# Layer 1's projections of the normalised input: fp16 pairs scaled on the chip in place of fp32r pairs

## The chip, the cores and the metric

The kernel runs on one core of one Trainium2 chip. The metric is the device time of one execution in microseconds (us); lower is better. TensorE is called PE in the profile (its weight loads PEld), VectorE DVE, ScalarE ACT, GpSimd POOL, and SyncE, which here only issues DMAs, SP.

## The reference, cut to what matters

Two layers of a diffusion trunk on 512 latent and 256 context tokens, 1024 channels. Each layer normalises its input, modulates it, multiplies it by one wide matrix `w_in` (1024 x 5376), runs two attentions (a neighbourhood attention A and a grouped-query attention B, 8 heads of 64 each), gates both, and projects twice.

```python
for l in range(2):
    mod_x = silu(c) @ w_ada + b_ada                       # likewise mod_c for the context
    hx = rmsnorm(x, norm_g) * (1 + scale_x) + shift_x      # hc for the context
    a_k, a_v, b_k, b_v, a_q, b_q, a_z, b_z, g_a, g_b = split(hx @ w_in)
    ca_k, ca_v, cb_k, cb_v = split(hc @ w_in)              # layer 1 needs no more of the context
    qa, ka, qb, kb = rmsnorm of each head of a_q, a_k, b_q, b_k (rotary on b)
    a_att, b_att = attention A, attention B
    o_a, o_b = (a_att * silu(a_z)) @ w_o_a, (b_att * silu(b_z)) @ w_o_b
    x = x + gate_x * ((sigmoid(g_a) * o_a + sigmoid(g_b) * o_b) @ w_out)
```

Everything is float32; the output is the latent stream after layer 1.

## The kernel before

To keep the accuracy of float32, each product of two matrices is three matmuls: each operand is split into a rounded part `hi` and a remainder `lo = value - hi`, and `mm3` adds hi*hi, hi*lo and lo*hi in one PSUM bank (L435, L436, L437). For all projections both parts are fp32r; for the attention values they are fp16 already.

Weights come in tiles of 128 x 512 float32. `load_w` (512 columns at once, one tile for each 128 rows) and `load_w2` (256 columns, two row blocks in one tile) issue the DMA from SP into one of three `raw` buffers (L403, L417), cast `whi` on ACT (L405, L420) and subtract `wlo` on DVE or POOL (L408, L422). `mix_lo` gives every second tile to POOL; `bq_lo` every fourth. There are eight `whi` and eight `wlo` buffers.

The input of a layer's projections, `hx`, is made by `make_hx` and `turn_hx`: one token tile at a time is normalised, transposed on PE, modulated on ACT (`modc` holds shift and scale by channel) and split by DVE (L350, L351). It takes four of the nine `big` buffers, two for `hi` and two for `lo`.

Two helpers run the projections. `tok_proj` has 128 tokens stationary and 512 or 256 weight columns moving, 24 matmuls a tile (8 row blocks, 3 each). `chan_proj` has 128 weight columns stationary and the tokens moving. In layer 1 these are: `a_k`, `a_v` (6 token tiles each, 512 wide), `b_k` with `b_v` (6 tiles, 256 wide), `a_q`, `b_q` (4 tiles each, 512 wide), and 24 pieces of `chan_proj`, 512 wide, for `a_z`, `b_z`, `g_a`, `g_b`.

A layer goes through these stages: A's projections; attention A, with gate pieces as filler on PE (`fill`, run by `pipeline`); the projections of B (`w = load_w2(W, C_BKV...)`, then `b_q`); attention B with more filler; and the merge, in which `o_chunks("b")` is projected by pieces, `evac_b` gates and adds on DVE, casts `mh` on ACT (L1223) and subtracts `ml` on DVE (L1224), and `w_out` is applied to the result (`tok_proj(w, 512, a_m, ...)`), in two halves of 512 columns. During layer 0's merge the modulation of layer 1 is computed on DVE from weights in `rawb` (`ada_steps`, L297; DMAs from POOL's queue, L290), ending in `ada_mod(1)`; while the second half of `w_out` runs, `make_hx(1, ...)` makes layer 1's input.

The program is recorded in this order, and a scheduler then sets the order of each engine's instructions from its own estimate of their times, bound by data, buffers and the few orders that `behind` fixes. An engine executes its own list in order.

`shrink`, `size` and `halves` exist before: for the attention values they find the largest magnitude over all partitions (a transpose and a one-column matmul on PE, five small DVE steps) and scale a tile so that it fits fp16.

Of the kernel before, what the change touches and what calls it, by code (L numbers as in the profile page):

```python
# [72 lines left out]
def hybrid_kernel(es: ExitStack, tc, x, ctx, cvec, w_ada, w_ada0, small, gvec, w_in, w_o_a, w_o_b, w_out,  # L73
# [112 lines left out]
    ehalf = cp.tile([128, 32], F32, name="ehalf")  # L186
    G.memset(ehalf, -0.5)

# [39 lines left out]

    modc = cp.tile([128, 2, 2, 16], F32, name="modc")

    def mod_finish(l, sums, k0, k1):
# [46 lines left out]
    def ada_steps(l, tiles, halves, nv, pool, queue=None):  # L278
# [58 lines left out]
    def turn_hx(l, t, y, h, hx, pool):  # L337

        v = 0 if t < 4 else 1
        full = pool.tile([128, 4, 128], F32, tag="half", name=nm("half"), bufs=2)  # L340
        pt = psw(512, "t")
        for k in range(4):
            T.transpose(pt[:, 128 * k:128 * k + 128], y[:, 512 * h + 128 * k:512 * h + 128 * k + 128], ident)
        for k in range(4):
            kk = 4 * h + k
            S.activation(full[:, k, :], pt[:, 128 * k:128 * k + 128], AF.Identity,
                         bias=modc[:, l, v, kk:kk + 1], scale=modc[:, l, v, 8 + kk:9 + kk])
        hi = hx[0][h].rearrange("p (k n) -> p k n", k=4)[:, :, 128 * t:128 * t + 128]
        lo = hx[1][h].rearrange("p (k n) -> p k n", k=4)[:, :, 128 * t:128 * t + 128]
        V.tensor_copy(R(hi), full)  # L350
        V.tensor_tensor(R(lo), full, hi, ALU.subtract)  # L351

# [43 lines left out]

    def load_w(src, col0, n, nk, lo_eng, k0=0, own=None, bufs=8):

        pool, x = (wp, "") if own is None else (own, "x")
        res = []  # L400
        for k in range(k0, k0 + nk):
            raw = raw_tile()
            nc.sync.dma_start(raw[:, :n], src[128 * k:128 * k + 128, col0:col0 + n])  # L403
            hi = pool.tile([128, 512], F32R, tag="whi" + x, name=nm("whi"), bufs=bufs)
# [7 lines left out]
    def load_w2(src, col0, nk, lo_eng):  # L412

        res = []
        for i in range(nk // 2):
            raw = raw_tile()
            nc.sync.dma_start(raw.rearrange("p (k n) -> p k n", k=2),  # L417
                              src[256 * i:256 * i + 256, col0:col0 + 256].rearrange("(k p) n -> p k n", k=2))
            hi = wp.tile([128, 512], F32R, tag="whi", name=nm("whi"), bufs=8)
            S.copy(hi, raw)  # L420
# [18 lines left out]
    def tok_mm(ps, w, n, a, t, k0, k1):  # L439
        for k in range(k0, k1):  # L440
            hi, lo = a(0, k), a(1, k)
            mm3(ps, (R(hi[:, 128 * t:128 * t + 128]), R(lo[:, 128 * t:128 * t + 128])),
                (w[k][0][:, :n], w[k][1][:, :n]), k == 0, k == KT - 1)
# [8 lines left out]
    def chan_proj(w, f, a, n0, n1, evac, late=0):  # L452
# [4 lines left out]
        wh = lambda k, i: w[k][i][:, 128 * f:128 * f + 128]  # L457
        act = lambda k, i: R(a(i, k)[:, n0:n1])
        for k in range(late):
# [34 lines left out]
    def open_heads(stack, name, bufs):  # L494
# [3 lines left out]
        for sq in hp["sq"]:  # L498
            V.memset(sq[:, :, HD:HD + 1], HD * EPS)

    def head_ss(ps, nh, ss):
# [93 lines left out]
    def layer(l, hx, nxt, start):  # L595
        first = l == 0
        ntok = NTOK if first else NLAT
        qt = 6 if first else 4
        a_hx = lambda part, k: hx_k(hx, part, k)
        spans = [(0, 512), (512, 768)] if first else [(0, 512)]  # L600
# [17 lines left out]
        def fill_chunks(col0, dst, spill, silu, eng):  # L618

            def evac(f, n0, n1, ps):  # L620
                if spill is None:
                    d = dst().rearrange("p (f n) -> p f n", f=4)[:, f, n0:n1]
                else:
                    d = ztp.tile([128, 512], F32, tag="zt", name=nm("zt"))[:, :n1 - n0]
                S.activation(d, ps, AF.Tanh, scale=0.5)  # L625
                if silu:
# [4 lines left out]
            for i in range(2):  # L631
                st = {}

                def ld(i=i, st=st):
                    st["w"] = load_w2(W, col0 + 256 * i, KT, eng)
                res.append((ld, [lambda f=f, n0=n0, n1=n1, i=i, st=st:
# [40 lines left out]
        def o_chunks(br, prepare, evac):  # L677

            src = (w_o_a if br == "a" else w_o_b)[l]
            act = lambda part, k: gated[br][part][:, k, :]  # L680
            res = []
# [53 lines left out]
        else:  # L735
            open_heads(bgp_es, f"cp{l}", 1)
            w = load_w(W, C_AK, 512, KT, mix_lo)
            hp["lag"] = 2
# [15 lines left out]
        def split_va():  # L754
            V.tensor_reduce(vmx[:, 6:7], vmx[:, 0:6], AX, ALU.max)
            shrink(vmx[:, 6:7], vsa, vsa[0:1, 2:3], 0.5 / P_UP)
            for t in range(0, 6, 2):
                halves(vf[:, t:t + 2, :].rearrange("p t (h d) -> p (t h) d", d=64),
                       va[:, t:t + 2].rearrange("p t h q d -> p (t h) q d"), vsa[:, 0:1])
        w = load_w(W, C_AV, 512, KT, mix_lo)  # L760
        for t in range(6):
# [8 lines left out]
        qav = big("qa").rearrange("p (j n) -> p j n", j=4)  # L770
        w = load_w(W, C_AQ, 512, KT, mix_lo, own=hp["p"])
        za = big("za")
# [18 lines left out]
        if True:  # L791
# [305 lines left out]
            def split_vb():  # L1097
                size(vf.rearrange("p t n -> p (t n)"), vbig[:, 1152:1920], vbig[:, 2946:2947])
                shrink(vbig[:, 2946:2947], vs, vbig[0:1, 2948:2949], 0.5)
                halves(vf.rearrange("p t (h d) -> p (t h) d", h=2), vb.rearrange("p t h q d -> p (t h) q d"),  # L1100
                       vs[:, 0:1])

            bg = gate_steps((0,), hp["p"]) if first else []
            w = load_w2(W, C_BKV, KT, mix_lo)
            w_q = []

            def load_q():
                w_q.extend(load_w(W, C_BQ, 512, 4, bq_lo) + load_w(W, C_BQ, 512, 4, bq_lo, 4, hp["p"], 4))
            if first:
# [98 lines left out]
        with tc.tile_pool(name=f"mrg{l}", bufs=1, reuse_waits="tile") as mp:  # L1208
# [33 lines left out]
            a_m = lambda part, k: mg[k // 4][part][:, k % 4, :]  # L1242
            bg = ada_steps(1, range(16), (1,), 2, mp, G) + [lambda: ada_mod(1)] if first else []
            run(bg, 1)
# [285 lines left out]
```

## Time and profile before

| | |
|---|---|
| three runs | 1105.44, 1108.48, 1111.61 us (median 1108.48) |
| the profiled execution | 1111.07 us, of which the span is 1109.3 us |
| granted TensorE clock, mean | 0.991 |
| PE, PEld busy | 1075.5 us (97%), 879.1 us (79%) |
| DVE, ACT, POOL busy | 767.4, 617.1, 473.1 us |
| DMA | 171.79 MB, mean 155 GB/s |

A row of a group names the line, the engine, the operation, the tiles (out<-in, buffer numbers left out) and the form, then the count, the busy time, the mean of one, and the idle time ahead of it with what ended it. In a timeline, a row has the start, the time that it took, and the same names; neighbours of one kind are merged with their count. The end of a matmul is modelled, so matmuls overlap in it: the distance between two starts is the cost of one, not its duration. In a table of windows, each row has a stretch, the busy time of each engine with its instructions, the granted clock, the mean busy share of the 16 DMA engines and what they moved.

### The profile page before, as it was taken

How to read it: one execution, taken by the hardware profiler on the slowest of the kernel's cores; microseconds unless marked ns; L12 is line 12 of the kernel's file. 1: busy time of each engine (PE TensorE's matmuls, PEld its weight loads, DVE VectorE, ACT ScalarE, POOL GpSimd, SP SyncE). 2: the span in 40 equal slices, each digit the busy share in tenths (PEclk: the TensorE clock that was granted, in tenths of full speed). 3: DMA queues.
4: the chain of work that ended last, by engine and by line, in shares of the span. 5: the costliest groups of instructions: out<-in, count | busy, mean ns of one | idle time of the engine just before them, and what ended most of it. 6: DMA issues, size and time to landing. Idle time of an engine off the chain costs nothing. (4 is left out here: it accounts for less than half of the span.)

```text
span 1109.3 us, 16937 instructions
## 1 busy us (share of the span) xinstructions
PE 1075.5 (97%) x5672; PEld 879.1 (79%) x5672; DVE 767.4 (69%) x1600; ACT 617.1 (56%) x1236; POOL 473.1 (43%) x397
## 2 busy tenths in 40 slices
PE   8999999999999989989999999999999999999998
PEld 5688888788888868767788878888877888777677
DVE  4667889975377487766777785366997665677473
ACT  6454279776433566765330275444899446786430
POOL 1054235555257154463621354232355472564531
PEclk9999999999999999998999999999999999999999
DMA  9455324554543379789633542453565536879642
GB/s 370 146 171 153 90 68 111 128 138 120 169 131 127 100 184 215 166 228 228 213 101 124 157 147 78 140 163 101 134 149 130 156 107 171 199 229 239 188 152 77
DMA packets 236000, 171.79 MB, mean 155 GB/s; under 512 B 160140, under 2 KB 201864, under 8 KB 234248
## 3 DMA queue, kind: packets, MB, share of 16 engines
q1 hardware_dynamic: 228576, 156.31, 51.6%
q0 software_dynamic: 2368, 7.87, 2.1%
q10 hardware_dynamic: 4968, 6.53, 1.8%
q8 instruction: 45, 0.74, 0.3%
q14 instruction: 43, 0.35, 0.1%
HBM read 115.58 MB, written 17.32 MB: 120 GB/s over the span
## 5 line engine op out<-in xcount | busy, mean ns | idle before, releaser
L842 POOL TENSOR_TENSOR h<-p,h 128x256 f16<-128x256 f32 (+2 forms) x104 | 113.6, 1101 | 160.0 <-ACT h L841 117.7
L422 POOL TENSOR_TENSOR wlo<-raw,whi 128x512 fp32r<-128x512 f32 x70 | 98.0, 1406 | 131.6 <-ACT whi L420 98.7
L435 PE MATMUL psf<-hx,whi 128*128 128x512 f32 (+1 forms) x360 | 138.2, 384 | 2.2 <-DVE zt L627 1.2
L436 PE MATMUL psf<-hx,whi 128*128 128x512 f32 (+1 forms) x360 | 136.1, 378 | 0.0
L437 PE MATMUL psf<-hx,wlo 128*128 128x512 f32 (+1 forms) x360 | 136.1, 378 | 0.0
L435 PE MATMUL psx<-whi,hx 128*128 128x512 f32 (+1 forms) x328 | 121.0, 372 | 0.0
L437 PE MATMUL psx<-whi,hx 128*128 128x512 f32 (+1 forms) x328 | 120.0, 367 | 0.0
L420 ACT CAST whi<-raw 128x512 fp32r<-128x512 f32 x136 | 83.2, 620 | 65.5 <-DMA raw<-in_w_in_dram 46.9
L436 PE MATMUL psx<-wlo,hx 128*128 128x512 f32 (+1 forms) x328 | 119.6, 366 | 0.0
L408 POOL TENSOR_TENSOR wlo<-raw,whi 128x512 fp32r<-128x512 f32 x40 | 59.8, 1499 | 117.7 <-ACT whi L405 74.6
L405 ACT CAST whi<-raw 128x512 fp32r<-128x512 f32 x88 | 54.3, 623 | 96.7 <-PE psx L437 34.2
L508 POOL TENSOR_TENSOR ss<-ss,ehalf 128x8 f32<-128x8 f32 (+2 forms) x40 | 63.6, 1593 | 77.2 <-DVE ss L505 72.2
L841 ACT CAST h<-p 128x256 f16<-128x256 f32 (+2 forms) x136 | 81.7, 616 | 5.3 <-DMA ht<-h 1.3
L422 DVE TENSOR_TENSOR wlo<-raw,whi 128x512 fp32r<-128x512 f32 x66 | 65.3, 992 | 25.9 <-ACT whi L420 24.3
L1161 DVE CUSTOM_DVE_ANT_0 p<-pss,vb 128x768 f32<-128x768 f32 x64 | 60.2, 953 | 31.0 <-PE pss L891 28.9
L1162 ACT ACTIVATE p<-pss,mx 128x768 f32<-128x768 f32 x64 | 57.6, 901 | 41.1 <-DVE mx L1161 40.4
L435 PEld LDWEIGHTS psf<-hx,whi 128*128 128x128 f32 x360 | 68.3, 190 | 14.9 <-ACT zt L625 1.9
L437 PEld LDWEIGHTS psf<-hx,wlo 128*128 128x128 f32 x360 | 68.2, 190 | 12.0
L436 PEld LDWEIGHTS psf<-hx,whi 128*128 128x128 f32 x360 | 68.3, 190 | 10.9
L437 PEld LDWEIGHTS psx<-whi,hx 128*128 128x128 f32 x328 | 61.9, 189 | 10.2
L436 PEld LDWEIGHTS psx<-wlo,hx 128*128 128x128 f32 x328 | 62.0, 189 | 9.5
L435 PEld LDWEIGHTS psx<-whi,hx 128*128 128x128 f32 x328 | 61.8, 189 | 9.1 <-issue 0.2
(338 smaller groups left out, 2984.7 us busy)
## 6 DMA issues: line engine op xcount, KB each, us to landing
raw<-in_w_in_dram SPq DMA_DIRECT2D x168, 256.0 KB, 3.0
rawb<-in_w_ada_dram SPq DMA_DIRECT2D x48, 256.0 KB, 2.8
raw<-in_w_out_dram SPq DMA_DIRECT2D x32, 256.0 KB, 2.9
tg<-gs SPq DMA_DIRECT2D x4, 1536.0 KB, 9.9
rawx<-in_w_ada_dram SPq DMA_DIRECT2D x4, 1024.0 KB, 10.3
rawy<-in_w_ada_dram SPq DMA_DIRECT2D x4, 1024.0 KB, 10.3
gs<-zt ACTq DMA_DIRECT2D x16, 256.0 KB, 2.6
raw<-in_w_o_a_dram SPq DMA_DIRECT2D x16, 256.0 KB, 3.1
```

Source lines behind the costliest of these rows:

```text
L405: S.copy(hi[:, :n], raw[:, :n])
L408: e.tensor_tensor(lo[:, :n], raw[:, :n], F(hi[:, :n]), ALU.subtract)
L420: S.copy(hi, raw)
L422: lo_eng(i).tensor_tensor(lo, raw, F(hi), ALU.subtract)
L435: T.matmul(ps, lhs[0], rhs[0], start=first, stop=False)
L436: T.matmul(ps, lhs[0], rhs[1], start=False, stop=False)
L437: T.matmul(ps, lhs[1], rhs[0], start=False, stop=last)
L508: G.tensor_tensor(ss, ss, ehalf[:, :n], ALU.pow)
L841: S.copy(h[:, 0], p[:, :n])
L842: eng.tensor_tensor(h[:, 1], p[:, :n], h[:, 0], ALU.subtract)
L1161: V.tensor_tensor_reduce(p, pss, lift, -1.0, 3e38, ALU.add, ALU.min, mx[:, 0:1])
L1162: S.activation(p, pss, AF.Exp, bias=mx[:, 0:1], accum_out=r[:, i:i + 1])
```

## The change

In layer 1 alone, `hx` and the weights of all its projections become pairs of fp16 tiles. Since fp16 has a narrow range, both are multiplied by a scale ahead of the split. The scale of the weights comes from a bound on them: ACT reads all of `w_in[1]` during layer 0, 64 blocks of 128 x 672, and adds up their magnitudes along each row (`bound_steps`); 36 blocks are read during layer 0's projections of B and 28 during its merge, and the largest row sum gives `s_w`. The scale of `hx` comes from the sum of the magnitudes of layer 1's modulation (`scale_mod`), and is multiplied into `modc`. Their product is divided out where it matters: in the scale of `Tanh`, in the scales of the values, and in the `eps` of the head norms (`set_eps`).

A weight tile is cast and scaled by one ACT instruction; the remainder is one `scalar_tensor_tensor` on DVE, or on POOL a `tensor_scalar` in place and then the subtraction. `hx` takes two `big` buffers in place of four. The blocks of the bound are read into a `big` buffer during B's projections and into an `extra` tile of the merge, four slots of each, by DMAs that ACT issues. The `rawb` tiles of the merge get four buffers in place of two.

```diff
+    s_w, dq = ehalf[:, 24:28], ehalf[:, 28:31]
+    def bound_steps(a, b, pool, space):
+        n = b - a
+        sums = pool.tile([128, n + 1], F32, tag="wsum", name=nm("wsum"), bufs=1)
+        def step(i):
+            k, c = i // 8, 672 * (i % 8)
+            t = space[:, 768 * (i % 4):768 * (i % 4) + 672]
+            S.dma_start(t, w_in[1][128 * k:128 * k + 128, c:c + 672])
+            S.activation(t, t, AF.Abs, accum_out=sums[:, i - a:i - a + 1])
...
+    def scale_mod(pool):
...
+        S.activation(t, m, AF.Abs, accum_out=s_h[:, 2:3])
+        shrink(s_h[:, 2:3], s_h, s_h[0:1, 3:4], 1.0)
+        V.tensor_scalar(m, m, s_h[:, 0:1], None, ALU.mult)
+        V.tensor_tensor(dq[:, 0:1], s_h[:, 1:2], s_w[:, 1:2], ALU.mult)
...
-            cb["w"] = pool.tile([128, 512], F32, tag="rawb", name=nm("rawb"), bufs=2)
+            cb["w"] = pool.tile([128, 512], F32, tag="rawb", name=nm("rawb"), bufs=4 if queue else 2)
...
-        V.tensor_copy(R(hi), full)
-        V.tensor_tensor(R(lo), full, hi, ALU.subtract)
+        hi, lo = [a[:, 4 * h:4 * h + 4, 128 * t:128 * t + 128] for a in hx]
+        V.tensor_copy(hi, full)
+        V.tensor_tensor(lo, full, hi, ALU.subtract)
...
+    def split_scaled(raw, pool, x, bufs, eng):
...
+        S.activation(hi, raw, AF.Copy, scale=s_w[:, 0:1])
+        if eng is V:
+            V.scalar_tensor_tensor(lo, raw, s_w[:, 0:1], hi, ALU.mult, ALU.subtract)
+        else:
+            G.tensor_scalar(raw, raw, s_w[:, 0:1], None, ALU.mult)
+            G.tensor_tensor(lo, raw, hi, ALU.subtract)
...
-                S.activation(d, ps, AF.Tanh, scale=0.5)
+                S.activation(d, ps, AF.Tanh, scale=0.5 if first else dq[:, 1:2])
...
+            wb = bound_steps(0, 36, hp["p"], big("wb")) if first else []
...
             for t in range(6):
                 tok_proj(w, 256, a_hx, t, evac_bkv)
...
+                run(wb, 2)
...
             for t in range(qt):
                 tok_proj(w_q, 512, a_hx, t, evac_bq)
                 run(bg, 2)
+                run(wb, 4 if t < 5 else len(wb))
...
+            wb = bound_steps(36, 64, mp, extra("wb")) + [bound_done] if first else []
             for i in range(4):
...
                 for piece in chunks[i][1]:
                     piece()
+                    run(wb, 2)
...
-            bg = ada_steps(1, range(16), (1,), 2, mp, G) + [lambda: ada_mod(1)] if first else []
+            bg = ada_steps(1, range(16), (1,), 2, mp, G) + [lambda: ada_mod(1), lambda: scale_mod(mp)] if first else []
...
-            hx1.extend([[big("hx") for _ in range(2)] for _ in range(2)])
+            hx1.extend([big("hx").bitcast(F16).rearrange("p (k n) -> p k n", k=8) for _ in range(2)])
```

Two places show what this does to the engines' lists. On PE, at the start of layer 1's `a_k` projection (`whi_7026` and `whi_7180` are the first weight tile, `hx_6680` and `hx_6836` the stationary `hi` part), before:

```order
L435 MATMUL psx_7072<-whi_7026,hx_6680 128x512
L435 MATMUL psx_7103<-whi_7026,hx_6680 128x512
L436 MATMUL psx_7072<-wlo_7028,hx_6680 128x512
L437 MATMUL psx_7072<-whi_7026,hx_6682 128x512
L436 MATMUL psx_7103<-wlo_7028,hx_6680 128x512
```

and now:

```order
L486 LDWEIGHTS hx_6836
L486 MATMUL psx_7263<-whi_7180,hx_6836 128x512
L487 LDWEIGHTS hx_6836
L487 MATMUL psx_7232<-wlo_7181,hx_6836 128x512
L488 LDWEIGHTS hx_6837
L488 MATMUL psx_7232<-whi_7180,hx_6837 128x512
```

An fp16 matmul has its weight load as an instruction of its own; the matmuls are as many as before.

On ACT, in layer 0's merge, from the last cast of attention B's gated output (`gbh`) on (`mh` are the casts of the merged result, `whi` the casts of weight tiles), before:

```order
L671 CAST gbh_5906<-zb_4067 128x256
L1223 CAST mh_5991<-tg_5318 128x512
L1223 CAST mh_5991<-tg_5318 128x256 x2
L1223 CAST mh_5991<-tg_5318 128x512
L1223 CAST mh_5991<-tg_5318 128x256 x2
L420 CAST whi_6143<-raw_6141 128x512
L420 CAST whi_6149<-raw_6147 128x512
L405 CAST whi_6304<-raw_6302 128x512
```

and now (`wb` are the blocks of the bound):

```order
L727 CAST gbh_5981<-zb_4142 128x256
L240 DMA wb_6054<-in_w_in_dram 128x672 x4
L241 ACTIVATE wb_6054,wsum_6055<-wb_6054 128x672
L1290 CAST mh_6068<-tg_5393 128x512
L240 DMA wb_6054<-in_w_in_dram 128x672
L1290 CAST mh_6068<-tg_5393 128x256 x2
L241 ACTIVATE wb_6054,wsum_6055<-wb_6054 128x672
L1290 CAST mh_6068<-tg_5393 128x512
L240 DMA wb_6054<-in_w_in_dram 128x672
L241 ACTIVATE wb_6054,wsum_6055<-wb_6054 128x672
L240 DMA wb_6054<-in_w_in_dram 128x672
L1290 CAST mh_6068<-tg_5393 128x256 x2
```

Between the casts that the merge needs stand reads of magnitudes, each behind its own DMA. Of the 28 blocks of this stage, 21 stand ahead of the last `mh` cast of 512 columns.

More of the change, by code (lines that the diff above doesn't have):

```diff
@@ L395, in split_lo, with load_w @@
         return hi, lo
-    def load_w(src, col0, n, nk, lo_eng, k0=0, own=None, bufs=8):
+    def split_scaled(raw, pool, x, bufs, eng):
+        n = raw.shape[-1]
+        hi = pool.tile([128, 512], F32, tag="whi" + x, name=nm("whi"), bufs=bufs).bitcast(F16)[:, :n]
+        lo = pool.tile([128, 512], F32, tag="wlo" + x, name=nm("wlo"), bufs=bufs).bitcast(F16)[:, :n]
+        S.activation(hi, raw, AF.Copy, scale=s_w[:, 0:1])
[4 more added lines that the diff above has]
+            G.tensor_tensor(lo, raw, hi, ALU.subtract)
+        return hi, lo
+    def load_w(src, col0, n, nk, lo_eng, k0=0, own=None, bufs=8, scaled=False):
         pool, x = (wp, "") if own is None else (own, "x")
@@ L403, in load_w @@
             nc.sync.dma_start(raw[:, :n], src[128 * k:128 * k + 128, col0:col0 + n])
+            if scaled:
+                res.append(split_scaled(raw[:, :n], pool, x, bufs, lo_eng(k)))
+                continue
             hi = pool.tile([128, 512], F32R, tag="whi" + x, name=nm("whi"), bufs=bufs)
@@ L410, in load_w, with load_w2 @@
         return res
-    def load_w2(src, col0, nk, lo_eng):
+    def load_w2(src, col0, nk, lo_eng, scaled=False):
         res = []
@@ L418, in load_w2 @@
                               src[256 * i:256 * i + 256, col0:col0 + 256].rearrange("(k p) n -> p k n", k=2))
+            if scaled:
+                hi, lo = split_scaled(raw, wp, "", 8, lo_eng(i))
+                res += [(hi[:, c:c + 256], lo[:, c:c + 256]) for c in (0, 256)]
+                continue
             hi = wp.tile([128, 512], F32R, tag="whi", name=nm("whi"), bufs=8)
@@ L634, in ld @@
                 def ld(i=i, st=st):
-                    st["w"] = load_w2(W, col0 + 256 * i, KT, eng)
+                    st["w"] = load_w2(W, col0 + 256 * i, KT, eng, not first)
                 res.append((ld, [lambda f=f, n0=n0, n1=n1, i=i, st=st:
@@ L756, in split_va @@
             shrink(vmx[:, 6:7], vsa, vsa[0:1, 2:3], 0.5 / P_UP)
+            if not first:
+                V.tensor_scalar(vsa[:, 1:2], vsa[:, 1:2], dq[:, 0:1], dq[:, 0:1], ALU.mult, ALU.mult)
             for t in range(0, 6, 2):
@@ L759, in split_va @@
                        va[:, t:t + 2].rearrange("p t h q d -> p (t h) q d"), vsa[:, 0:1])
-        w = load_w(W, C_AV, 512, KT, mix_lo)
+        w = load_w(W, C_AV, 512, KT, mix_lo, scaled=not first)
         for t in range(6):
@@ L770, in layer @@
         qav = big("qa").rearrange("p (j n) -> p j n", j=4)
-        w = load_w(W, C_AQ, 512, KT, mix_lo, own=hp["p"])
+        w = load_w(W, C_AQ, 512, KT, mix_lo, own=hp["p"], scaled=not first)
         za = big("za")
```

42 lines of the change are left out of this document (31 added, 11 removed).

## The prediction

> **What bounds the kernel now.** I read the page's head first, then a table of windows for the stages that the change touches, then the waits of PE.
>
> ```profile
> span 1109.3 us, 16937 instructions
> PE 1075.5 (97%) x5672; PEld 879.1 (79%) x5672; DVE 767.4 (69%) x1600; ACT 617.1 (56%) x1236; POOL 473.1 (43%) x397
> core 0: us, PE busy (x) PEld busy (x) DVE busy (x) ACT busy (x) POOL busy (x), PEclk, DMA share, GB/s
> 300.00:364.00 64.00, 64.00 (x375) 55.89 (x375) 46.55 (x96) 25.15 (x53) 35.00 (x27) 1.00 0.41 131
> 549.00:588.00 39.00, 39.00 (x221) 34.17 (x220) 30.68 (x55) 13.71 (x26) 8.17 (x7) 1.00 0.43 153
> 547.00:557.00 10.00, 10.00 (x59) 8.72 (x58) 5.06 (x12) 2.39 (x5) 2.91 (x4) 1.00 0.92 337
> 577.00:587.00 10.00, 10.00 (x52) 8.46 (x51) 10.00 (x19) 4.28 (x8) 1.30 (x1) 1.00 0.41 132
> 664.00:760.00 96.00, 96.00 (x448) 79.02 (x447) 52.12 (x97) 42.90 (x79) 35.65 (x24) 1.00 0.42 127
> 800.00:840.00 40.00, 39.60 (x207) 31.58 (x206) 38.79 (x107) 38.51 (x86) 18.98 (x22) 1.00 0.59 133
> 875.00:916.00 41.00, 41.00 (x217) 34.71 (x216) 28.81 (x51) 18.63 (x39) 28.59 (x23) 1.00 0.36 110
> ```
>
> The stages are layer 0's projections of B (300 to 364) and merge (549 to 588), and layer 1's projections of A (664 to 760), attention A (800 to 840 lies in it) and projections of B (875 to 916). PE is busy in all of the projections, at the full clock. So a matmul that costs less there shortens the kernel, and work given to ACT costs nothing as long as it fits beside. The exceptions: at 800 to 840 DVE and ACT have 39 of 40 us too, and at 577 to 587 DVE has no idle time at all.
>
> **What the matmuls give back.** A matmul's cost is the distance to the next start:
>
> ```profile
> 702.51 0.39 PE L435 MATMUL psf<-whi,hx 128*128 128x512 f32 x1
> ...
> 707.05 0.39 PE L437 MATMUL psf<-whi,hx 128*128 128x512 f32 x1
> 1007.95 0.38 PE L1179 MATMUL pst<-ht,vb 128*128 128x512 f16 x1
> ...
> 1010.11 0.38 PE L1179 MATMUL pst<-ht,vb 128*128 128x512 f16 x1
> 878.09 0.28 PE L436 MATMUL psx<-wlo,hx 128*128 128x256 f32 x1
> ...
> 879.05 0.28 PE L435 MATMUL psx<-whi,hx 128*128 128x256 f32 x1
> 254.78 0.27 PE L1007 MATMUL psv<-pt,va 128*128 128x256 f16 x1
> 254.89 0.27 PE L1011 MATMUL psv<-pt,va 128*128 128x256 f16 x1
> ```
>
> From 702.51 to 707.05 there are 20 steps: 0.227 us for an fp32r matmul of 512 columns. From 1007.95 to 1010.11 there are 10: 0.216 us in fp16, with a weight load ahead of each, as the changed projections have it. For 256 columns it is 0.96 us over 8 steps, 0.120, against 0.11. Layer 1 has 24 x (6 + 6 + 4 + 4) = 480 matmuls of `a_k`, `a_v`, `a_q`, `b_q` and 24 x 24 = 576 of the gate pieces, 1056 of 512 columns, and 24 x 6 = 144 of 256. That is 1056 x 0.011 = 11.6 us and 144 x 0.010 = 1.4 us: **13 us** at most. Some of the 576 are filler where DVE and ACT are as full as PE (800 to 840), so a faster piece may only end in a wait; I take 1 us off, and count **12** (10 to 13).
>
> **The reads of the bound, on ACT.** No instruction of before has their form, 128x672 with a sum. Its neighbours:
>
> ```profile
> 225.03 0.72 ACT L984 ACTIVATE p<-p,mx 128x512 f32<-128x512 f32 x1 [1.10 <-DVE mx L981]
> 225.66 0.19 ACT L984 ACTIVATION_READ_ACCUMULATOR p<-p,mx 128x1 f32 x1
> 225.75 0.71 ACT L984 ACTIVATE p<-p,mx 128x512 f32<-128x512 f32 x1
> 635.90 1.06 ACT L330 ACTIVATE full<-xt 128x1024 f32<-128x1024 f32 x1 [9.58 <-DVE xt L1254]
> 636.87 0.18 ACT L330 ACTIVATION_READ_ACCUMULATOR full<-xt 128x1 f32 x1
> 359.63 0.33 ACTq L629 DMA_DIRECT2D gs<-zt  x1
> raw<-in_w_in_dram SPq DMA_DIRECT2D x168, 256.0 KB, 3.0
> tg<-gs SPq DMA_DIRECT2D x4, 1536.0 KB, 9.9
> ```
>
> With its sum, 512 columns take 0.72 us from start to start (225.03 to 225.75) and 1024 take 0.97 + 0.09 = 1.06; 672 lie at 0.72 + 160/512 x 0.34 = 0.83. Each also has a DMA issue of 0.33 on ACT's queue. Where that issue refills the slot which the read just ahead of it frees, ACT's list waits for it; most do, so I count it in full. A block of 336 KB lands in 3.4 us between the two DMA rows (3.0 + 80/1280 x 6.9), more where the engines are full: 0.92 busy at 337 GB/s makes 366 GB/s the full rate.
>
> *Layer 0's merge.* The end of this stage hangs on a chain without slack:
>
> ```profile
> 553.02 0.62 ACT L1223 CAST mh<-tg 128x512 fp32r<-128x512 f32 x1 [3.73 <-DVE tg L1221]
> 587.19 0.62 ACT L1223 CAST mh<-tg 128x512 fp32r<-128x512 f32 x1 [1.51 <-DVE tg L1221]
> 588.01 1.02 DVE L1224 TENSOR_TENSOR ml<-tg,mh 128x512 fp32r<-128x512 f32 x2
> 589.03 0.39 PE L437 MATMUL psx<-whi,ml 128*128 128x512 f32 x1
> ```
>
> The last wide cast `mh` starts at 587.19, DVE subtracts from 588.01 to 589.03, and PE has begun `w_out` meanwhile and takes the result at once. A late cast holds DVE, which executes in order and frees the PSUM banks, and so PE. From 553.02 to the end of that cast ACT has 34.8 us. In it now go 13.3 us of casts (the 13.71 of the window, less what lies before 553), 21 reads, 17.4, and 21 issues, 6.9: 37.6 us, **2.8 too many**. The DMAs agree: 39 us at 153 GB/s are 6.0 MB, and 25 blocks of 0.344 MB (21 read, 4 under way) add 8.6; 14.6 MB at 366 GB/s are 39.9 us. From below: with all issues under other work nothing is late, 0. From above: if a block takes 5 us to land in this crowd, four slots give one block in (5 + 0.83 + 0.33)/4 = 1.54 us, 21 in 32.3, and if no cast fits into these waits, 45.6 us, 11 late. I take **3**, the plain sum, as the casts stand between the reads in ACT's list. The last seven blocks and the scale have the first half of `w_out` ahead of them, 6 x 24 x 0.227 = 33 us, before `s_w` is wanted; nothing.
>
> *Layer 0's projections of B.* ACT has 25.15 us in 64. With 36 reads (29.9) and issues (11.9) it has 66.9; the first four blocks can be read before 300, as their slots are empty early, which takes off 3.3. So ACT is full to the brim, the DMAs are not (8.4 MB + 12.4 MB in 57 us). PE runs ahead of ACT's evacuation by up to six PSUM banks, 2.9 us each in `b_k` (24 x 0.120) and 5.4 in `b_q`, and the weight casts of `b_q` stand ahead of 22 of the reads. If that cover fails, by the rate of 1.54 us a block the stage is 32 x 1.54 + 25 - 64 = 10 us late. I take **1.5** (0 to 10).
>
> **Layer 1's weights and input.** 84 weight tiles are split; 40 of them on POOL, which now does two instructions:
>
> ```profile
> L422 POOL TENSOR_TENSOR wlo<-raw,whi 128x512 fp32r<-128x512 f32 x70 | 98.0, 1406 | 131.6 <-ACT whi L420 98.7 <-PE psf L436 12.0 <-PE psx L436 11.9
> L842 POOL TENSOR_TENSOR h<-p,h 128x512 f16<-128x512 f32 x8 | 10.8, 1347 | 8.3 <-ACT h L841 6.4 <-issue 1.9
> L331 POOL TENSOR_SCALAR ss<-ss x6: 234/458/692, 637.1 to 658.7; 128x1 f32<-128x1 f32 x6
> L798 ACT ACTIVATE p<-p,r 128x512 f32<-128x512 f32 x32 | 22.7, 720 | 2.6 <-DVE r L794 2.1 <-DVE r L795 0.4
> L420 ACT CAST whi<-raw 128x512 fp32r<-128x512 f32 x136 | 83.2, 620 | 65.5 <-DMA raw<-in_w_in_dram 46.9 <-DMA raw<-in_w_o_a_dram 5.5 <-DMA raw<-in_w_o_b_dram 3.7
> 642.52 0.18 DVE L306 TENSOR_TENSOR as<-asum 128x32 f32<-128x32 f32 x1
> ```
>
> The subtraction stays (1.35 against 1.41). The scaling of 512 columns costs between 0.23 (one column) and 1.41 (two inputs): I take 0.9, 36 us in all, and each of the three `raw` buffers, and with it SP's list behind the next load, is held that much longer on every second tile. POOL has 36 us of 96 and 29 of 41 in the two projection stages; eight tiles hold four scalings, 3.6 us, against 24 x 6 x 0.216 = 31 us of PE's work. ACT's scaled cast costs 0.1 more than the plain one. All hidden, **0**; without that cover, six changes of weights at 1 us each, 6. The scale of `hx` adds about eight small steps behind `ada_mod(1)`, which begins at 642.52 today; the deeper `rawb` lets these sums end sooner. **0** (-1 to 2).
>
> **Sum.** -12 + 3 + 1.5 = -7.5 us. Against the profiled execution's own 1111.07 us this is 1103.6; that execution lay near the top of the three runs (1105.44 to 1111.61), so I forecast 1108.48 - 7.5 = **1101** as the median.
>
> **The rivals.**
>
> 1. *The reads become the bound of layer 0's two stages* (slower). If blocks land in 5 us and not 3.4, ACT's ordered list waits for each, with casts and squares behind it: 11 + 10 us against 12 gained, 1108.5 + 9 = 1117. It decides from the point where both stages together lose over 12 us. For it: the crowded DMAs at 547 to 557, ACT's sums of 38 in 35 and 64 in 64. Against it: four blocks in flight, PSUM banks ahead. The Trainium skill (DMA: Bandwidth & Descriptors, "Issuing engines are not separate DMA queues") says that DMAs issued from different engines run on the same 16 engines, so ACT's own queue brings no bandwidth of its own; no row before shows two loaded queues together. Chance 0.26.
> 2. *POOL becomes late with weights in layer 1*: half of the gain is eaten, 1108.5 - 7.5 + 6 = 1107. For it: DMAs to three `raw` buffers set the pace of the casts (L420 idles 46.9 us for them). Against: PE there waits for no weight tile today. Chance 0.12.
> 3. *The fp16 projections are spaced like the fp32r ones*, so the change doesn't do what it is made for: 1108.5 + 4.5 = 1113. Only matmuls of attention values have shown 0.216 so far. The Trainium skill (TensorE: Matmul & The Clock Gate, "Back-to-back issue gap") gives N/2.4 + 2.5 ns, 216 ns for 512 columns, and names no type; by that rule fp32r has nothing to lose to fp16. The trace has it for fp16 alone: 0.216, and 0.227 for fp32r. Chance 0.05.
> 4. *Everything hides*: 1108.5 - 13 = 1095.5. Chance 0.11.
>
> **How the numbers follow.** The forecast keeps 0.46, with a range of its own of 1096 to 1106. Measurement can tell about 0.5%, 5.5 us, from no change, so faster means below 1102.9 and slower above 1114. Faster: 0.33 of the forecast's 0.46 and all of rival 4, 0.44. Same: 0.13 of the forecast, 0.11 of rival 2, 0.05 of rival 1, 0.02 of rival 3, 0.31. Slower: 0.21, 0.03 and 0.01 of rivals 1, 3 and 2, 0.25. The range is 1094 to 1119: it holds all but the far ends of rivals 1 and 4.
>
> **What would show it.** Right: starts 0.216 us apart in layer 1's projections, no waits for weight tiles there, `w_out` of layer 0 begun about 4.5 us later than before, layer 1 shorter by 12. Wrong: ACT idle on `wb` DMAs for more than a few us with PE waiting behind it; PE waiting for POOL's `wlo` in layer 1; or a spacing of 0.227. Attention stages that lose time because the scheduler ordered them anew would be a cause that I have not priced.

## The result, and the profile after

The changed kernel takes 1135.7 us (median of five runs, 1134.1 to 1136.9) against 1108.5 before: 2.4% slower, ratio 1.024 with a 95% interval of 1.022 to 1.027. The forecast was 1101, and its range ended at 1119.

The head of the page after, of an execution of 1136.2 us:

```profile
span 1134.5 us, 17231 instructions
PE 1072.5 (95%) x5678; PEld 784.7 (69%) x5678; DVE 781.6 (69%) x1621; ACT 676.2 (60%) x1366; POOL 536.7 (47%) x437
```

PE is busy 3 us less than before, in a span that is 25 us longer; POOL is busy 64 us more. The matmuls did become cheaper. The question is who holds PE up.

The windows of layer 1's four stages say where. Before (A's projections, attention A, B's projections, attention B up to the last `w_out`):

```profile
core 0: us, PE busy (x) PEld busy (x) DVE busy (x) ACT busy (x) POOL busy (x), PEclk, DMA share, GB/s
653.00:748.00 95.00, 95.00 (x448) 78.27 (x447) 54.94 (x95) 48.36 (x95) 36.63 (x26) 1.00 0.43 128
748.00:865.00 117.00, 114.81 (x590) 91.98 (x590) 95.21 (x248) 90.66 (x194) 50.76 (x52) 1.00 0.53 131
865.00:906.00 41.00, 41.00 (x254) 36.44 (x253) 29.98 (x57) 19.95 (x44) 24.89 (x22) 1.00 0.40 125
906.00:1059.00 153.00, 149.53 (x701) 114.81 (x701) 99.47 (x157) 97.77 (x173) 79.67 (x54) 1.00 0.77 198
```

and after:

```profile
657.00:753.00 96.00, 92.09 (x449) 45.22 (x448) 55.66 (x93) 51.33 (x97) 59.84 (x41) 0.98 0.40 121
753.00:878.00 125.00, 114.89 (x595) 62.48 (x594) 99.93 (x255) 94.78 (x195) 72.72 (x65) 0.99 0.50 127
878.00:916.00 38.00, 38.00 (x254) 24.76 (x252) 26.69 (x58) 19.34 (x41) 28.68 (x24) 1.00 0.45 134
916.00:1084.00 168.00, 151.35 (x701) 95.05 (x699) 109.70 (x159) 102.16 (x177) 95.12 (x64) 0.97 0.74 180
```

B's projections are 3 us shorter, as forecast. A's are not shorter at all, attention A is 8 us longer and attention B 15, with PE idle and its granted clock below 1 in just these three. POOL has 60 us in place of 37 in A's projections. (The prediction's windows for layer 1 lay about ten us late: its 664 to 760 begins inside A's projections and ends in attention A.)

For every kernel below, the table gives the stages by the distance in us between the first matmuls of one stage and the next, to about half a us, from the trace of one execution of each; "to `w_out`" is attention B and the merge of layer 0. B's projections of layer 0 are within 52.8 to 53.0 us in all. The runs were on several chips, where the kernel before took 1108.0 to 1109.5 us, so a ratio is always to the kernel before on the same chip; where two changed kernels are compared by their medians, the comparison by the ratios can differ by 2 us.

| kernel | median | to w_out (0) | w_out (0) | A proj. | att. A | B proj. | att. B |
|---|---|---|---|---|---|---|---|
| before | 1108.5 | 230.4 | 70.0 | 94.5 | 117.2 | 41.0 | 153.3 |
| after | 1135.7 | 235.8 | 68.7 | 95.7 | 124.5 | 38.0 | 168.5 |
| four big buffers | 1127.2 | 234.8 | 68.6 | 96.4 | 125.0 | 38.4 | 159.8 |
| splits on DVE only | 1117.0 | 234.8 | 68.6 | 89.8 | 121.8 | 40.6 | 158.3 |
| both of these | 1112.0 | 235.1 | 70.7 | 90.2 | 120.5 | 40.1 | 152.6 |
| both, no reads | 1108.5 | 230.2 | 68.4 | 89.3 | 122.3 | 40.6 | 153.5 |
| no reads | 1128.3 | 228.7 | 68.4 | 96.1 | 123.1 | 38.0 | 167.7 |
| unscaled, four big | 1098.8 | 228.7 | 68.3 | 89.3 | 117.8 | 37.9 | 152.0 |
| unscaled, two big | 1112.5 | 228.8 | 68.4 | 89.3 | 117.3 | 37.9 | 164.9 |
| before + reads | 1126.3 | 235.1 | 77.7 | 97.0 | 118.1 | 41.0 | 153.0 |
| before + reads, 4 `rawb` | 1113.6 | 233.4 | 70.5 | 94.8 | 117.4 | 41.0 | 152.9 |
| before + POOL | 1133.0 | 228.4 | 69.0 | 96.4 | 122.7 | 54.0 | 158.4 |
| before + POOL behind | 1116.4 | 228.8 | 68.4 | 95.7 | 123.5 | 41.1 | 153.0 |
| both + idle POOL | 1116.5 | 234.4 | 69.3 | 89.8 | 123.6 | 41.7 | 152.2 |

Kernels that leave layer 0 as it was show 228.4 to 230.4 in the first column, so differences of 2 us mean nothing there.

**Where PE waits.** In A's projections PE, whose waits before add up to nothing, stops once, at 731. The timeline of PE:

```profile
731.18 0.38 PE L488 MATMUL psx<-whi,hx 128*128 128x512 f16 x1
735.38 0.27 PE L622 MATMUL pst<-ident,vmx 128*1 128x128 f32 x1 [3.82 <-DVE vmx L812]
...
735.72 0.63 PE L487 MATMUL psx<-wlo,hx 128*128 128x512 f16 x1
736.15 0.63 PE L488 MATMUL psx<-whi,hx 128*128 128x512 f16 x1
...
739.12 0.38 PE L486 MATMUL psx<-whi,hx 128*128 128x512 f16 x1
739.33 0.38 PE L487 MATMUL psx<-wlo,hx 128*128 128x512 f16 x1
```

A transposition of 128 x 1 (`vmx`, the maximum for the values' scale) stands in PE's list ahead of weight tiles that are ready, and it waits for DVE. DVE's timeline just ahead of it:

```profile
731.06 0.69 DVE L330 CUSTOM_DVE_ANT_0 rawb<-rawb,cb 128x512 f32<-128x512 f32 x1 [1.18 <-DMA rawb<-in_w_ada_dram]
...
734.46 0.69 DVE L330 CUSTOM_DVE_ANT_0 rawb<-rawb,cb 128x512 f32<-128x512 f32 x1 [0.58 <-DMA rawb<-in_w_ada_dram]
```

DVE waits for transfers of `rawb`, which SP issues from the same list as the weight loads. This batch of them begins 66 us into the stage (723.6), against 62 before (715.4). That POOL is what makes them late is not shown by SP's waits: the weight loads wait about as long in total for `raw` buffers before (29.1 us for POOL's remainders, 12.4 for DVE's) as now (14.8 and 30.5). Run 2, without POOL's splits, is the test. The stop costs its 4 us and something more: the matmuls behind it start 0.43 us apart until 739.1, then 0.216. The windows show the granted clock of these four us:

```profile
735.00:739.00 4.00, 3.62 (x10) 1.43 (x11) 1.63 (x7) 1.93 (x3) 0.38 (x1) 0.58 0.81 254
739.00:743.00 4.00, 4.00 (x21) 2.05 (x20) 2.42 (x3) 1.30 (x2) 3.92 (x3) 0.99 0.62 188
```

The clock is 0.58 after the stop and 0.99 four us later: eight matmuls at double their price, 1.7 us. The Trainium skill (TensorE: Matmul & The Clock Gate, "HAM oscillation — how this bites in real kernels") warns of idle gaps over about 3.4 us on PE, after which the clock falls to half; the gap here, 4.2 us from start to start and 3.8 of them idle, agrees. At 762.7 the same happens again (4.1 us, for `ag`, behind the last `rawb` tile).

In attention B of layer 1, POOL's timeline shows what stands between the last two rope steps of `b_q` (L644), and the rows of DVE and PE show who waits for it:

```profile
917.00 1.27 POOL L728 TENSOR_TENSOR gal<-za,gah 128x512 fp32r<-128x512 f32 x1
...
920.28 4.62 POOL L728 TENSOR_TENSOR gal<-za,gah 128x512 fp32r<-128x512 f32 x3
924.88 3.10 POOL L437 TENSOR_SCALAR raw<-raw,ehalf 128x512 f32<-128x512 f32 x2
927.95 1.26 POOL L644 TENSOR_TENSOR ry<-ry,tabs 128x512 f32<-128x512 f32 x1
929.24 0.69 DVE L647 TENSOR_TENSOR rr<-rr,ry 128x512 f32<-128x512 f32 x1 [5.47 <-POOL ry L644]
930.08 0.95 PE L585 MATMUL pst<-ident,rr 128*128 128x128 f32 x4 [2.13 <-DVE rr L647]
```

The operand `ry` was ready at 922, when DVE had read it for the last time; POOL takes it at 927.95, behind the rest of the four `gal` and two scalings. `gal` splits attention A's gated output for a product that comes much later. Before, these four ran at 985 to 989:

```profile
L672 POOL TENSOR_TENSOR gal<-za,gah x4: 1267/1370/1716, 984.9 to 988.8; 128x512 fp32r<-128x512 f32 x4
```

On SP's queue the load that follows them waits:

```profile
SPq L731 <- POOL gal L728: 20.5, 1, 20.5
```

For these 20.5 us no weight load behind it is issued. Two things come together here: POOL's second instruction, and `gal` standing almost 70 us earlier than before. Runs 1, 2, 5 and 9 take them apart.

### The profile page after: what moved, and what is told of

It is laid out like the page before. It is cut to its first block, busy times and chain, and to the rows that moved or that the text cites. A ratio compares the mean times of both kernels' runs of the same rounds, so it can differ in the third digit from the quotient of the medians.

```text
span 1134.5 us, 17231 instructions
## 1 busy us (share of the span) xinstructions
PE 1072.5 (95%) x5678; PEld 784.7 (69%) x5678; DVE 781.6 (69%) x1621; ACT 676.2 (60%) x1366; POOL 536.7 (47%) x437
## 5 line engine op out<-in xcount | busy, mean ns | idle before, releaser
L901 POOL TENSOR_TENSOR h<-p,h 128x256 f16<-128x256 f32 (+2 forms) x104 | 115.7, 1120 | 143.2 <-ACT h L900 112.5
L486 PE MATMUL psf<-hx,whi 128*128 128x512 f32 (+2 forms) x360 | 136.8, 380 | 3.9 <-ACT zt L681 2.6
L488 PE MATMUL psf<-hx,wlo 128*128 128x512 f32 (+2 forms) x360 | 135.8, 377 | 1.0 <-POOL wlo L438 1.0
L487 PE MATMUL psf<-hx,whi 128*128 128x512 f32 (+2 forms) x360 | 135.3, 376 | 0.0
L488 PE MATMUL psx<-whi,hx 128*128 128x512 f32 (+3 forms) x328 | 119.1, 363 | 0.0
L486 PE MATMUL psx<-whi,hx 128*128 128x512 f32 (+3 forms) x328 | 119.0, 365 | 0.0
L487 PE MATMUL psx<-wlo,hx 128*128 128x512 f32 (+3 forms) x328 | 118.8, 362 | 0.1
L473 POOL TENSOR_TENSOR wlo<-raw,whi 128x512 fp32r<-128x512 f32 x44 | 62.1, 1416 | 78.1 <-ACT whi L471 48.8
L433 ACT ACTIVATE whi<-raw,ehalf 128x512 f16<-128x512 f32 x84 | 59.5, 720 | 63.0 <-DMA raw<-in_w_in_dram 58.9
L564 POOL TENSOR_TENSOR ss<-ss,ehalf 128x8 f32<-128x8 f32 (+2 forms) x40 | 65.4, 1638 | 64.5 <-DVE ss L561 61.8
L437 POOL TENSOR_SCALAR raw<-raw,ehalf 128x512 f32<-128x512 f32 x40 | 67.6, 1690 | 49.5 <-ACT whi L433 47.7
L455 POOL TENSOR_TENSOR wlo<-raw,whi 128x512 fp32r<-128x512 f32 x26 | 41.4, 1596 | 101.3 <-ACT whi L452 57.3
L486 PE MATMUL psx<-hx,whi 128*128 128x256 f32 (+2 forms) x208 | 68.2, 328 | 0.0
L488 PE MATMUL psx<-hx,wlo 128*128 128x256 f32 (+2 forms) x208 | 67.5, 325 | 0.0
L487 PE MATMUL psx<-hx,whi 128*128 128x256 f32 (+2 forms) x208 | 67.5, 324 | 0.0
L949 PE MATMUL pss<-gk,qs 128*128 128x256 f32 (+1 forms) x144 | 53.4, 376 | 6.9 <-ACT p L1229 4.6
```

The source lines that it names most:

```text
L433: S.activation(hi, raw, AF.Copy, scale=s_w[:, 0:1])
L437: G.tensor_scalar(raw, raw, s_w[:, 0:1], None, ALU.mult)
L473: lo_eng(i).tensor_tensor(lo, raw, F(hi), ALU.subtract)
L486: T.matmul(ps, lhs[0], rhs[0], start=first, stop=False)
L487: T.matmul(ps, lhs[0], rhs[1], start=False, stop=False)
L488: T.matmul(ps, lhs[1], rhs[0], start=False, stop=last)
```

## The experiments

**1. hx in four big buffers.** The fp16 `hx` fills two big buffers where fp32r filled four, so two are free and a tile that waits for one (`gah`, `gal`, `tg`) can start earlier. The edit takes four again, each half full:

```diff
-  hx1.extend([big("hx").bitcast(F16).rearrange("p (k n) -> p k n", k=8) for _ in range(2)])
+  hx1.extend([[big("hx").bitcast(F16)[:, :3072].rearrange("p (k n) -> p k n", k=4) for _ in range(2)] for _ in range(2)])
```

> Layer 1's hx stays in fp16 but takes four big buffers again, each half full; nothing else is edited. Theory B (two freed big buffers let the four subtractions gal and the loads tg of attention B's stage start in the middle of the last q rope steps, on POOL and on SP's queue): the stage from the end of b_q to w_out of layer 1, 168.5 us in the changed kernel, falls to about 152, the rest stays, and the time is about 1119 us. Theory P (POOL's two instructions for a weight tile are what is late): this edit leaves POOL's load alone, so the stage stays above 163 and the time above 1130. Theory R (the reads of the bound): no change, 1135.

Measured 1127.2 (ratio to before 1.017, 1.015 to 1.019): 8.5 us off, all of it in attention B (168.5 to 159.8). Theory B holds in place and sign, at half of the size expected: 6 us of that stage's loss stay.

**2. The splits on DVE.** One `scalar_tensor_tensor` for all 84 tiles:

```diff
-        if eng is V:
+        if True:
             V.scalar_tensor_tensor(lo, raw, s_w[:, 0:1], hi, ALU.mult, ALU.subtract)
```

> All 84 scaled weight tiles are split on DVE, in one instruction each, none on POOL; the reads and the two freed big buffers stay. Theory P: the 4 us stalls of PE in layer 1's projections of A go, attention A of layer 1 falls from 124.5 us to about 115, in all 12 to 15 us less, 1121. Theory B: attention B's stage stays near 168 and the time falls by less than 6, to about 1131. If DVE, with about 40 us more, becomes the bound instead, the time is above 1135.

Measured 1117.0 (1.009, 1.007 to 1.010): 18.7 us off, more than expected. A's projections fall to 89.8, the whole gain of the matmuls; attention B falls by 10, though `gal` stands as early as in the changed kernel (909 to 915 us, in a stage that begins at 908). Attention A stays 4.6 us above before, and B's projections give back 2.6 of their 3.

**3. No reads of the bound.** No block is read; a constant stands for the largest row sum, and the scale is made from it as before:

> The 64 reads of the bound and their DMAs are left out; the scale of the weights comes from a constant in place of the largest row sum. Theory R as in the prediction's first rival (reads cost layer 0 about 21 us): 1115. By the stages of the changed kernel's profile, which put only about 5 us more into layer 0, 1130 to 1131; theories B and P both say the same 1131, since neither is touched.

Measured 1128.3 (1.019, 1.017 to 1.021), 7.4 us off, nearly all in layer 0. The prediction's first rival, which puts 21 us on the reads in these stages, is out for the changed kernel.

**4. The kernel before with the reads.**

> The kernel before with the 64 reads of the bound added in layer 0, where the changed kernel has them, and the bound then not used; all fp32r pairs stay. By the stages of the changed kernel's profile 1113 (5 us more, all of it in layer 0 before w_out); by the prediction's sum 3 + 1.5 = 4.5 us more; by rival 1 1129.

Measured 1126.3 (1.016, 1.013 to 1.018), 18 us more and not 5. The stages that hold most of the reads grew by 4.7 us, as expected; from `w_out` of layer 0 to layer 1's input, where the last of them stand, it takes 77.7 us in place of 70. PE waits there once for long. ACT's rows ahead of it, and PE's:

```profile
599.19 0.76 ACT L241 ACTIVATE wb<-wb 128x672 f32<-128x672 f32 x1 [4.01 <-DMA wb<-in_w_in_dram]
599.95 0.60 ACT L1248 CAST mh<-tg 128x512 fp32r<-128x512 f32 x1
600.60 0.79 PE L457 MATMUL psx<-whi,mh 128*128 128x512 f32 x1 [4.76 <-ACT mh L1248]
```

This is the chain of the prediction, and its sign of being wrong: ACT waits for a block, a cast `mh` stands behind the read, and PE waits for the cast. The granted clock is 0.80 around it (594 to 601). The kernel before has two `rawb` buffers in this stage, the changed kernel four, and run 10 tests that difference. DVE's wait for `rawb` is no explanation by itself: it adds up to 9.1 us here, and to 8.3 in the kernel before.

**5. Both edits of 1 and 2.**

> Both edits at once, four big buffers for hx and all scaled weight tiles split on DVE; the reads of the bound stay. If the two costs are separate, as theories B and P have it, they add up: 8.5 + 18.7 us off the changed kernel's 1135.7, 1108.5, and attention B's stage of layer 1 at 150 us, below the 153.3 of the kernel before. If both remove the same wait (POOL's queue at the last rope steps), it stays at 1115 and the stage at 157.

Measured 1112.0 (1.003, 1.002 to 1.005), between the two expectations. Attention B is back at 152.6. The two costs are mostly separate, and overlap by some 3.5 us.

**6. Both edits and no reads.**

> As the one before, and without the reads of the bound (a constant in place of the largest row sum). If the reads cost 7 us here too, as they did in the changed kernel, 1101; the start of w_out in layer 0 near 580 us. If the reads are hidden once POOL is not late, as the one before, 1108.

Measured 1108.5 (1.000, 0.998 to 1.002). The reads cost 3.5 us here. Nothing is left of POOL's second instruction, of the freed buffers and of the reads, and still there is no gain over before: attention A takes 122.3 us.

**7. No scaling of the weights.** fp16 pairs of the weights as they are, the split by one plain cast and one subtraction on DVE or POOL as in the kernel before, `hx` in four big buffers and no reads; the guard against weights outside the range of fp16 is left out.

```diff
-        S.activation(hi, raw, AF.Copy, scale=s_w[:, 0:1])
+        S.copy(hi, raw)
...
-            G.tensor_scalar(raw, raw, s_w[:, 0:1], None, ALU.mult)
             G.tensor_tensor(lo, raw, hi, ALU.subtract)
```

> fp16 pairs with the weights not scaled at all: no reads of the bound, the scale of the weights is 1, a weight tile is cast plainly on ACT and subtracted once on DVE or POOL, as in the kernel before; hx is scaled as in the changed kernel, in four big buffers. What is left is the spacing of the matmuls: by the prediction's count 12 us less than before, 1096.5. If the gate pieces' 6 us give nothing, because DVE and ACT set the pace of the attention stages (theory A), 7 less, 1101. If the two attention stages lose time even so, something in the fp16 pairs themselves is slow, 1108 or more.

Measured 1098.8 (0.993, 0.991 to 0.995): faster than both kernels, and by 7.8 us than the one before, by the ratio (5.3 to 10.2). The windows of layer 1's four stages:

```profile
649.00:739.00 90.00, 90.00 (x449) 44.88 (x448) 52.51 (x96) 48.43 (x95) 34.63 (x27) 1.00 0.45 134
739.00:856.00 117.00, 111.90 (x585) 61.00 (x584) 94.56 (x250) 92.04 (x194) 49.51 (x52) 1.00 0.52 133
856.00:894.00 38.00, 38.00 (x259) 25.21 (x257) 27.01 (x58) 18.16 (x42) 21.32 (x20) 1.00 0.42 127
894.00:1046.00 152.00, 147.39 (x703) 93.89 (x702) 102.31 (x157) 99.50 (x176) 80.62 (x56) 1.00 0.78 199
```

PE's busy time falls by 3 us in attention A and 2 in attention B, and neither stage gets shorter by as much, as theory A has it (that DVE and ACT set the pace there is read from the windows and not tested). In the projections the whole gain arrives. Beside it the window of attention A in run 6, where DVE scales all tiles:

```profile
741.00:863.00 122.00, 112.16 (x585) 61.05 (x583) 100.70 (x262) 94.57 (x194) 34.54 (x40) 0.99 0.51 130
```

DVE has 100.7 us there in place of 94.6. Runs 6 and 7 differ by 9.7 us (7.5 by the ratios), and that is the price of scaling when DVE does it: the longer cast on ACT, and 40 splits more on DVE. Which of the two it is, no run separates.

**8. The kernel before with POOL's extra instruction.** All fp32r, no reads, no scale; each of the 40 weight tiles of layer 1 on POOL is multiplied by one ahead of its subtraction:

```diff
+            if e is G and src is twice[0]:
+                G.tensor_scalar(raw, raw, ehalf[:, 24:25], None, ALU.mult)
             e.tensor_tensor(lo, raw, F(hi), ALU.subtract)
```

> The kernel before, fp32r throughout, but each of layer 1's 40 weight tiles on POOL is first multiplied by one in place, with the instruction that the changed kernel has there. Theory P: the projections of A, attention A and attention B of layer 1 get longer by 5, 4 and 9 us, in all about 1126. If POOL has room, as the prediction had it (0, and 6 without cover): 1108 to 1114.

Measured 1133.0 (1.023, 1.020 to 1.025): 24.6 us from this alone, above the 1126 of theory P, and not in its places. Attention A and attention B are 5.5 and 5.1 us longer, A's projections 2, and 13 us stand in B's projections (54.0 against 41.0), where the changed kernel loses nothing (38.0). There PE stops for 5.0 us, at 878.8, ahead of attention A's last value products (L1011), which now stand behind the first matmuls of B's projections; the profile doesn't name what it waits for. So POOL had no room for the instruction, but the 24.6 us are not what it costs in the changed kernel.

**9. Unscaled, with two big buffers free.** Run 7 with `hx` as in the changed kernel:

> As the unscaled run, but hx takes two big buffers as in the changed kernel, so that two are free. Theory B: the subtractions gal stand again between the last rope steps of b_q, and attention B's stage of layer 1, 152.0 us with four, is 5 to 9 us longer (5.7 was the difference with DVE doing the splits, 8.7 in the changed kernel); time 1104 to 1108. If the freed buffers hurt only where POOL is loaded twice, no difference, 1099.

Measured 1112.5 (1.004, 1.002 to 1.005), 13.7 us more than run 7 by the medians and 11.6 by the ratios, and all of it in attention B: 164.9 against 152.0. POOL and PE there:

```profile
894.11 1.26 POOL L727 TENSOR_TENSOR gal<-za,gah 128x512 fp32r<-128x512 f32 x1
897.39 4.62 POOL L727 TENSOR_TENSOR gal<-za,gah 128x512 fp32r<-128x512 f32 x3
914.18 0.63 PE L584 MATMUL pst<-ident,rr 128*128 128x128 f32 x4 [3.33 <-DVE rr L646]
```

Two buffers more, and the kernel is 1.1% slower: the freed space lets the scheduler start work that nobody needs yet on a queue that others need now. The lists themselves show it. POOL's, at the last rope steps, in run 7:

```order
L643 TENSOR_TENSOR ry_9675<-ry_9675,tabs_9247 128x512
...
L643 TENSOR_TENSOR ry_9729<-ry_9729,tabs_9247 128x512
L643 TENSOR_TENSOR ry_9774<-ry_9774,tabs_9247 128x512
...
L727 TENSOR_TENSOR gal_10570<-za_7596,gah_10569 128x512 x4
```

and in this one:

```order
L643 TENSOR_TENSOR ry_9673<-ry_9673,tabs_9245 128x512
L727 TENSOR_TENSOR gal_10568<-za_7594,gah_10567 128x512
...
L727 TENSOR_TENSOR gal_10568<-za_7594,gah_10567 128x512 x3
...
L643 TENSOR_TENSOR ry_9727<-ry_9727,tabs_9245 128x512
...
L643 TENSOR_TENSOR ry_9772<-ry_9772,tabs_9245 128x512
```

**10. Before with the reads and four `rawb` buffers.**

> The kernel before with the reads, as in the earlier run that took 18 us more, but with four buffers for rawb in the merge, as the changed kernel has. Theory Q (the reads crowd the DMAs of the modulation's weights, which two buffers cannot cover): w_out of layer 0 to layer 1's input takes 70 us again in place of 77.7, and the time is about 1118. If the reads themselves cost the 18 us, 1126.

Measured 1113.6 (1.004, 1.002 to 1.005): 4 us over before (2.6 to 5.3), against 18 with two buffers. PE's wait of 4.8 us is gone. The list is another one, too: the last wide cast `mh` stands ahead of the read that waits.

```profile
593.76 0.63 ACT L1248 CAST mh<-tg 128x512 fp32r<-128x512 f32 x1 [0.24 <-DVE tg L1246]
596.21 0.77 ACT L241 ACTIVATE wb<-wb 128x672 f32<-128x672 f32 x1 [1.82 <-DMA wb<-in_w_in_dram]
```

Two buffers more take away some 14 us; whether by the buffers themselves or by the order that came with them stays open.

**11. Idle work on POOL.** Run 5 with two instructions on POOL for each of the 40 tiles, which read the finished remainder; POOL is then as busy as in the changed kernel (543 against 537 us over the span).

> As the run with four big buffers and all splits on DVE (1112.0), with two idle instructions on POOL for each of the 40 tiles that POOL had in the changed kernel: they read the finished remainder and write a free part of an hx buffer, and nobody waits for them but POOL's own list. Theory P1 (POOL's time is what costs: its list also holds the head norms, the rope and softmax steps): about as slow as the changed kernel with four buffers, 1125. Theory P2 (the late remainder and the raw buffer held longer cost): no change, 1112.

Measured 1116.5 (1.006, 1.005 to 1.008): 4.5 us more than run 5 by the medians and 3.2 by the ratios, 3 of them in attention A. With four big buffers, POOL's splits cost 15 us in all (runs 1 and 5), so POOL's time alone is the smaller part.

**12. POOL's extra instruction behind the subtraction.** Run 8 with its two POOL instructions in the other order:

> The kernel before, with the 40 multiplications on POOL behind the subtraction and not ahead of it: the raw buffer is held as long as in the run that took 1133.0 us, and POOL has as much to do, but the remainder is ready 1.7 us earlier. If what costs is the buffer held longer, with SP's loads behind it (theory P2a), about 1130. If it is the remainder that is late for PE (theory P2b), about 1113, what POOL's time alone costs.

Measured 1116.4 (1.007, 1.005 to 1.008): 8 us over before, against 24.6 with the multiplication ahead. Of the 16.6 us that this order saves, 13 are those of B's projections (41.1 again) and 5 are in attention B (153.0 again), so there it is the multiplication ahead of the result that costs. Attention A keeps its 6 us more (123.5): there it is POOL's time or the `raw` buffer that is held, as in run 11, and the changed kernel loses 7 us in that stage. What this does not separate is the order of the lists: the scheduler made other lists from each of the two programs, and a remainder that is later for it moves other work too.

## Why the prediction was wrong

Two of its terms failed: the price and the cover of POOL's second instruction, and the two freed buffers, which had no term.

- *What the matmuls give back*: right for the projections. The spacing is 0.216, rival 3 is out. In run 7 A's projections are 5.2 us shorter and B's 3.1, where the count gave 4.2 and 2.5 (384 and 96 of 512 columns, 144 of 256). Of the gate pieces' 576 x 0.011 = 6.3 us I took 1 off; measured are 0.7 us of gain in both attention stages together. The step that failed in this term is to read the fullness of DVE and ACT from the one window 800 to 840 and then charge only 1 us for it. The 12 are 8 to 10.
- *The reads*: right in size, 4.5 forecast, 4.0 in run 10, 3.5 between runs 5 and 6, 7.4 between the changed kernel and run 3. That is luck: the terms were off and made up for each other. In ACT's timeline a read's step is 0.75 us (346.50 to 347.25) and not 0.83, and its DMA issue mostly runs beside the work that is under way, here a copy, where I counted 0.33 in full (of ACT's idle time ahead of the 64 reads, 14.5 us is for blocks that have not landed, and 1.9 for all else):

```profile
344.80 0.57 ACT L599 COPY qb<-pst 128x512 f32<-128x512 f32 x1
344.92 0.33 ACTq L240 DMA_DIRECT2D wb<-in_w_in_dram  x1
...
346.50 0.76 ACT L241 ACTIVATE wb<-wb 128x672 f32<-128x672 f32 x1
...
347.25 0.76 ACT L241 ACTIVATE wb<-wb 128x672 f32<-128x672 f32 x1
```

  A block lands in 4.8 us, not 3.4. The place was off too. In the merge, which had 3 of the 4.5 us, PE waits for nothing (553 to 589). B's projections keep their 53.0 us (I had given them 64), and the delay comes just behind them, where PE waits for the last `rr`, made from squares that stand between the reads in ACT's list. The row of the DMAs, and PE's timeline:

```profile
wb<-in_w_in_dram ACTq DMA_DIRECT2D x64, 336.0 KB, 4.8
356.20 0.63 PE L585 MATMUL pst<-ident,rr 128*128 128x128 f32 x4 [0.99 <-DVE rr L647]
...
366.61 0.70 PE L585 MATMUL pst<-ident,rr 128*128 128x128 f32 x4 [1.90 <-DVE rr L642]
```

- *The deeper `rawb`*, costed at "0 (-1 to 2)" for the end of the sums, goes with reads that are cheap: with two buffers they cost 18 us (run 4), with four 4 (run 10).
- *Layer 1's weights*: "all hidden, 0", and 6 without cover, is the step that failed worst. The price was low, the cover was the wrong one. POOL's group of scalings and its subtractions behind them, in the changed kernel:

```profile
L437 POOL TENSOR_SCALAR raw<-raw,ehalf 128x512 f32<-128x512 f32 x40 | 67.6, 1690 | 49.5 <-ACT whi L433 47.7 <-issue 1.7
L438 POOL TENSOR_TENSOR wlo<-raw,whi 128x512 f16<-128x512 f32 x40 | 51.4, 1289 | 1.7
```

  The scaling takes 1.69 us; I took 0.9 between ends of 0.23 and 1.41 and held the two-input instruction for an upper end. And the cover was counted as free time (36 of 96 us) and as the distance to the next weights. But POOL's list also carries the head norms' power (L564), one of the two products of the rope (L644) and most of the softmax remainders (L901), each with DVE and then PE behind it, in an order that is fixed before the run. An engine that is idle for half of the time can still be late for the step that is waited for. Rival 2 had the engine right, and asked only for weights that PE waits for; it was priced at 6 us. In the changed kernel PE waits only 1.0 us for a remainder that POOL scaled; what comes late are the other steps of its list. Taking POOL's splits out gains 19 in the changed kernel (run 2) and 15 with four big buffers (runs 1 and 5). With all splits on DVE instead, scaling still costs 9.7 (runs 6 and 7); the scaled cast on ACT was in this 0 too.
- *hx in two buffers*: told in the change, and not priced at all. It costs 8.5 us in the changed kernel (run 1) and 12 to 14 without the other loads (run 9). The prediction named attention stages that are ordered anew as a cause it had no price for. The lists, which show `gal` between the rope steps, were not read at that place.
- Together, taken off the changed kernel one after the other, by the medians: POOL's splits and the freed buffers 23.7 us (run 5), the reads 3.5 (run 6), the scaling 9.7 (run 7), 36.9 in all. The matmuls give back 9.7 (run 7 against before). The difference is the 27.2 us that were measured.

## What to carry to other kernels

Count an instruction on a half-idle engine by what stands behind it in that engine's list, not by the engine's free time: here 1.7 us on each of 40 tiles cost the kernel before 25 us, and 8 in lists where it stood behind the result that was waited for. Freed memory is a change of the order too: where buffers hold a scheduler back, giving some back can start work early on queues that the critical path needs, and keeping the old footprint gained 8.5 us in the changed kernel and 12 to 14 in the unscaled one. And a faster matmul pays where PE alone is full, in the projections; the version that keeps the splits as they were and scales nothing is the one that gained (1098.8 us), without the guard on the range.

## What was not expected of the hardware

POOL's one-input multiplication by a column, in place (1.55 us at least, 1.69 in the mean for 128 x 512 in float32), is slower than its two-input subtraction (1.29). The Trainium skill (GPSIMD Engine Reference, "4.1 Engine selection") has one-input operations roughly at line rate and two-input ones at twice the cost of DVE; the trace says otherwise for this form, and DVE does the scaling and the subtraction in one instruction of 0.96 in the mean (0.75 the median). A stop of PE of about 4 us costs 1.7 us more than itself, in matmuls at a clock of 0.58 over the next 4 us.
